# Forming the recurrence's level scores for all blocks of a chunk in one batch per level

## The chip, the cores and the metric

The kernel runs on one core of a Trainium2 chip. The metric is the device time of one execution in microseconds, as the median of several runs. The core has five engines with queues of their own, which run in order and wait for each other by semaphores: PE (TensorE, matrix products, with its weight loads shown as PEld), DVE (VectorE), ACT (ScalarE), POOL (GpSimd) and SP (SyncE, which here issues most DMAs).

## The reference

One layer of a hybrid decoder runs for a prompt of 1024 tokens and a sample group of 8 sequences with 8 new tokens each (64 rows). It is a SwiGLU feed-forward, then a mixer, then another feed-forward. The mixer projects the normed input once and splits the columns between sliding-window attention and a gated linear recurrence (HGRN2) with 4 heads, 128 keys and 128 values. What matters here is the recurrence:

```python
hq = jax.nn.silu(hq)
f = lb + (1.0 - lb) * jax.nn.sigmoid(hf)
o, S = hgrn2_chunked(hq, 1.0 - f, jnp.log(f), hi, s0)
...
def step(S, inp):
    qb, kb, gb, vb = inp
    G = jnp.cumsum(gb, axis=2)
    diff = G[:, :, :, None, :] - G[:, :, None, :, :]
    decay = jnp.exp(jnp.where(causal, diff, -jnp.inf))
    A = jnp.einsum('bhtk,bhsk,bhtsk->bhts', qb, kb, decay)
    o = jnp.einsum('bhts,bhsv->bhtv', A, vb) + jnp.einsum('bhtk,bhkv->bhtv', qb * jnp.exp(G), S)
    G_last = G[:, :, -1:, :]
    S = jnp.exp(G_last[:, :, 0, :])[..., None] * S + jnp.einsum('bhsk,bhsv->bhkv', kb * jnp.exp(G_last - G), vb)
    return S, o
```

So inside a block every query `t` meets every earlier key `s` with the product of the forget gates between them, per key dimension; across blocks a state of 128 x 128 per head is carried.

## The kernel before

The 1088 tokens are cut into three chunks (`WIDTH`): chunk 0 has two prompt blocks of 128 and the 64 sample rows, chunks 1 and 2 have three prompt blocks each (`NPB`). Weights and activations of the large products are split into a high and a low part, and `mm3` (L277 to L281) makes three products of each pair, which is where L279, L280 and L281 come from. The program runs feed-forward 1, the mixer's projection `w_in_units`, the mixer, the output projection `w_out_units` and feed-forward 2, with the chunks staggered.

Work that is small but long in dependence (norms, the attention, the recurrence) is written as generators. `stream` starts one with a rate, `tick` is called between pieces of the large products and advances every running stream by its rate in steps (one step ends at a `yield`), and `need` drains a stream before its result is used. `mixer(n)` (L1495) of chunk `n` alternates between a chain of attention steps and a chain of recurrence steps; its rates are `RM = [0.95, 1.0, 1.3]`. The order on each engine's queue is then made by the framework's scheduler, which places instructions by a simulated time; the queues are fixed in the built program.

The recurrence takes the blocks one after another: `hgrn_block` (L1311), and `sample_hgrn` (L1424) for the sample rows. Both begin with `intra` (L1230), which forms the matrix `At` of scores inside a block. The product of gates between key `s` and query `t` is built up by levels: at level `h` (1, 2, 4, ... 64) the block is cut into pairs of runs of `h` tokens, and queries in the second run of each pair meet keys in the first. `Q` and `K` hold queries and keys scaled so far, and `Ds` the gate products over runs of 1, 2, 4, ... tokens. One step of the ladder is:

- PE: the products of `K` and `Q`. Up to `h = 16` all products inside 32 x 32 diagonal squares are formed (`blocks`, L1245, 4 heads x 4 squares, the tile `lv`), and for `h = 32` and `64` just the rectangles that are wanted (L1274, tile `l`). Before the ladder the diagonal itself is formed from unscaled keys and queries (tile `ld`), together with level 1.
- DVE: `copy_predicated` (L1269) takes from the squares what belongs to level `h` into `C`; then `Q` is scaled (L1285).
- POOL: `K` is scaled (L1287); at the end `C` is copied into `At` (L1280). POOL also makes `Ds` (L1259) and clears `At` (L1241).
- ACT: copies `K` out of the chunk's keys at the start (L1239) and the rectangles into `At` (L1277).

Every step ends at a `yield`. After the ladder the block's keys are transposed (L1323), the output is formed from `At`, the values, `Q` and the state (L1329, L1332), and the state is updated (L1336, L1341).

Tiles come from pools with a fixed count of slots: `big` has 12 slots of 6 KB per partition, and holds the projected `q`, `k`, `f`, `hq`, `v` and `g` of a chunk among others; `t2` has 8 slots of 2 KB, where `Q`, `K` and `D` of a block lie; `At` has one slot and `C` two. PSUM has four banks for large products (`mm`) and four for all else (`ax`).

Of the kernel before, what the change touches and what calls it, by code (L numbers as in the profile page):

```python
# [8 lines left out]
F32 = mybir.dt.float32  # L9
# [36 lines left out]
def tile_step(ctx: ExitStack, tc: tile.TileContext, A: dict, O: list):  # L46
# [996 lines left out]
    def mixing(tp, h):  # L1043
# [16 lines left out]
        Z, KX, VN, MT = {}, {}, {}, {}  # L1060
# [169 lines left out]
        def intra(n, c0, r, top, last_q, res):  # L1230

            z = Z[n]
            f, k, q = [z[i][:, :, c0:c0 + r] for i in ("f", "k", "hq")]
            Q, K, D = t2((P, 4, P)), t2((P, 4, P)), t2()
            V.tensor_tensor(Q[:, :, :r], q, f, op=ALU.mult)
            S.copy(K[:, :, :r], k)  # L1239
            At = tp.tile([P, 4, P], F32, tag="At", bufs=1, name=uid("At"))  # L1240
            G.memset(At, 0.0)  # L1241
            C = tp.tile([P, 4, 32], F32, tag="cm", bufs=2, name=uid("cm"))
            nq = r // 32

            def blocks(s, *pairs):  # L1245
                b5 = axbank(s).rearrange("p (l a t) -> p l a t", l=4, a=4)
                for n_, (x, y) in enumerate(pairs):
                    for a in range(4):
                        for i in range(nq):
                            cs = slice(32 * i, 32 * i + 32)  # L1250
                            PE.matmul(b5[cs, n_, a], x[:, a, cs], y[:, a, cs], start=True, stop=True)  # L1251
                return b5

            Ds, off, h = [f], 0, 1
            while h <= top:
                nx = r // (2 * h)
                Dv = Ds[-1].rearrange("p a (x e) -> p a x e", e=2)
# [3 lines left out]
                h *= 2  # L1261
# [4 lines left out]
            while h <= top:  # L1266
                if h <= 16:
                    b4 = b5[:, 1] if h == 1 else blocks("lv", (K, Q))[:, 0]
                    V.copy_predicated(C[:r], lmask[h][:r].unsqueeze(1).to_broadcast([r, 4, 32]), b4[:r])  # L1269
                else:  # L1270
                    b4 = axbank(f"l{h}").rearrange("p (a t) -> p a t", a=4)
                    for c in range(0, r, 2 * h):
                        for a in range(4):
                            PE.matmul(b4[c:c + h, a, :h], K[:, a, c:c + h], Q[:, a, c + h:c + 2 * h],  # L1274
                                      start=True, stop=True)
                    for c in range(0, r, 2 * h):
                        S.copy(At[c:c + h, :, c + h:c + 2 * h], b4[c:c + h, :, :h])  # L1277
                if h == min(top, 16):
                    for i in range(nq):
                        G.tensor_copy(At[32 * i:32 * i + 32, :, 32 * i:32 * i + 32], C[32 * i:32 * i + 32])  # L1280
                nx = r // (2 * h)
                Qv, Kv = [t[:, :, :r].rearrange("p a (x u) -> p a x u", u=2 * h) for t in (Q, K)]
                Dv = Ds.pop(0).rearrange("p a (x e) -> p a x e", e=2)
                if last_q or h < top:
                    V.tensor_tensor(Qv[:, :, :, h:], Qv[:, :, :, h:], Dv[:, :, :, 0:1].to_broadcast([P, 4, nx, h]),  # L1285
                                    op=ALU.mult)
                G.tensor_tensor(Kv[:, :, :, :h], Kv[:, :, :, :h], Dv[:, :, :, 1:2].to_broadcast([P, 4, nx, h]),  # L1287
                                op=ALU.mult)
                h *= 2
                yield  # L1290
            res += [At, Q, K, Ds[0]]
# [19 lines left out]
        def hgrn_block(n, b):  # L1311
# [6 lines left out]
            res = []  # L1318
            yield from intra(n, c0, P, 64, not first, res)
            At, Q, K, D = res  # L1320
            tb = axbank("kT").rearrange("p (a t) -> p a t", a=4)
            for a in range(4):
                PE.transpose(tb[:, a], K[:, a], ident)  # L1323
# [4 lines left out]
            for a in range(4):  # L1328
                PE.matmul(ob[:, a * P:(a + 1) * P], At[:, a], z["v"][:, b, a * P:(a + 1) * P],  # L1329
                          start=True, stop=first)  # L1330
                if not first:
                    PE.matmul(ob[:, a * P:(a + 1) * P], Q[:, a], st[:, a], start=False, stop=True)  # L1332
# [6 lines left out]
            else:  # L1339
                for a in range(4):  # L1340
                    V.scalar_tensor_tensor(st[:, a], st[:, a], D[:, a], ub[:, a],  # L1341
# [82 lines left out]
        def sample_hgrn():  # L1424
            n, c0, r = 0, 256, NS
            z = Z[n]
            res = []
            yield from intra(n, c0, r, 4, True, res)
            At, Q, K, D = res
            tb = axbank("skT").rearrange("p (a t) -> p a t", a=4)  # L1430
            for a in range(4):
                PE.transpose(tb[:r, a], K[:, a, :r], ident)
# [3 lines left out]
            for a in range(4):  # L1436
# [3 lines left out]
                G.tensor_tensor(qm, Q[:, a, :r].rearrange("p (f t) -> p f t", f=2).unsqueeze(2).to_broadcast(  # L1440
# [312 lines left out]
```

## Time and profile before

| | |
|---|---|
| runs (3) | median 1992.44 us, 1992.08 to 1993.96 |
| profiled execution, first to last instruction | 1991.5 us |
| mean granted TensorE clock of the profiled execution | 0.999 |
| DMA, bytes moved and mean rate | 370.31 MB, 186 GB/s |
| HBM read, written | 284.31 MB, 84.71 MB |

For the profiled execution there is its span alone; the runs' times hold what lies around the span too. The profile counts an instruction as busy from its start to its modelled end, and products of PE overlap, so the start of one to the start of the next tells more of PE than the busy time. A product of two plain float32 operands leaves two records in the trace, one of the high and low parts leaves one. "idle before, releaser" names what the engine waited for.

### The profile page before, as it was taken

To read this page: it belongs to the slowest core of one execution; us is meant where nothing else is said; L and a number is where in the kernel's file an instruction comes from. 1 tells how busy PE (TensorE), PEld (TensorE's weight loads), DVE (VectorE), ACT (ScalarE), POOL (GpSimd) and SP (SyncE) were. 2 spreads that over 40 slices of the span, in tenths; PEclk is the share of its full clock that TensorE was granted. 3 is DMA by queue.
4 is the path that set the end of the run, shared out by engine and by line. 5 is a ranking of instruction groups with operands and counts; after the bars stand their busy time and mean duration, and the time that the engine had idled before them with its cause. 6 is when DMAs were issued, how large, how long until landed. Compare 5 with 4: busy or idle time off the path is not lost.

```text
span 1991.5 us, 34618 instructions
## 1 busy us (share of the span) xinstructions
PE 1978.7 (99%) x13331; PEld 1854.6 (93%) x13331; DVE 1406.9 (71%) x2595; ACT 949.0 (48%) x1736; POOL 178.0 (9%) x244
## 2 busy tenths in 40 slices
PE   9999999999999999999999999999999999999998
PEld 8999999999998987797999898989999999999886
DVE  7686767886558656777667756756887877655667
ACT  5753334444445444445344444756544444444453
POOL 0000000000004101211113311220000000000201
PEclk9999999999999999999999999999999999999999
DMA  8735555755677647766434343527565555677874
GB/s 230 225 107 186 175 170 177 232 196 192 228 243 212 182 138 236 251 169 181 128 104 132 92 138 107 177 90 237 165 210 191 197 183 193 209 232 232 291 262 140
DMA packets 377319, 370.31 MB, mean 186 GB/s; under 512 B 40546, under 2 KB 294321, under 8 KB 377137
## 3 DMA queue, kind: packets, MB, share of 16 engines
q1 hardware_dynamic: 371169, 357.21, 56.9%
q10 hardware_dynamic: 5984, 10.88, 1.6%
q8 instruction: 105, 1.72, 0.4%
q14 instruction: 61, 0.50, 0.1%
HBM read 284.31 MB, written 84.71 MB: 185 GB/s over the span
## 4 chain that ended last, share of the span: by engine, by line
PE 96%; DMA 1%; DVE 1%; ACT 1%; issue 0%; SPq 0%; DVEq 0%; ACTq 0%
PE mm L279 28%; PE mm L280 28%; PE mm L281 28%; PE pv L1219 1%; PE c L281 1%; PE c L279 1%; PE c L280 1%; PE sc L1178 1%; PE pT L1206 1%; PE tr L511 1%; DMA ar<-fa 1%; PE lv L1251 1%; PE l L1274 0%; DMA raw<-in_ffn_w_gu_dram 0%; DMA xt<-in_x_prompt_dram 0%; PE av L1329 0%
## 5 line engine op out<-in xcount | busy, mean ns | idle before, releaser
L279 PE MATMUL mm<-h,wsph 128*128 128x320 f32 (+1 forms) x1280 | 407.3, 319 | 0.0
L280 PE MATMUL mm<-h,wsph 128*128 128x320 f32 (+1 forms) x1280 | 405.3, 317 | 0.0
L281 PE MATMUL mm<-h,wspl 128*128 128x320 f32 (+1 forms) x1280 | 403.6, 317 | 0.0
L258 ACT CAST wsph<-raw 128x1024 fp32r<-128x1024 f32 x200 | 209.1, 1048 | 269.6 <-PE mm L280 213.7
L259 DVE TENSOR_TENSOR wspl<-raw,wsph 128x1024 fp32r<-128x1024 f32 x200 | 247.7, 1240 | 125.3 <-ACT wsph L258 120.7
L258 ACT CAST w<-raw 128x512 fp32r<-128x512 f32 (+1 forms) x218 | 160.3, 740 | 209.2 <-PE mm L280 111.9
L259 DVE TENSOR_TENSOR w<-raw,w 128x512 fp32r<-128x512 f32 (+1 forms) x218 | 185.8, 856 | 87.6 <-ACT w L258 87.1
L279 PEld LDWEIGHTS mm<-h,wsph 128*128 128x128 f32 x1280 | 240.2, 188 | 3.8 <-issue 2.8
L281 PEld LDWEIGHTS mm<-h,wspl 128*128 128x128 f32 x1280 | 239.9, 188 | 2.8 <-issue 2.3
L280 PEld LDWEIGHTS mm<-h,wsph 128*128 128x128 f32 x1280 | 240.5, 188 | 1.5 <-issue 1.1
L279 PE MATMUL mm<-h,w 128*128 128x384 f32 (+1 forms) x720 | 240.3, 335 | 0.6 <-ACT w L258 0.5
L280 PE MATMUL mm<-h,w 128*128 128x384 f32 (+1 forms) x720 | 240.7, 335 | 0.0
L281 PE MATMUL mm<-h,w 128*128 128x384 f32 (+1 forms) x720 | 235.4, 334 | 0.0
L279 PE MATMUL mm<-w,h 128*128 128x512 f32 x462 | 181.1, 395 | 0.6 <-DVE big L975 0.6
L280 PE MATMUL mm<-w,h 128*128 128x512 f32 x462 | 181.3, 392 | 0.0
L281 PE MATMUL mm<-w,h 128*128 128x512 f32 x462 | 179.8, 391 | 0.0
L280 PE MATMUL mm<-big,w 128*128 128x384 f32 x528 | 176.5, 334 | 0.0
L279 PE MATMUL mm<-big,w 128*128 128x384 f32 x528 | 176.3, 334 | 0.0
L281 PE MATMUL mm<-big,w 128*128 128x384 f32 x528 | 176.2, 334 | 0.0
L279 PEld LDWEIGHTS mm<-h,w 128*128 128x128 f32 x720 | 135.0, 188 | 1.3 <-ACT w L258 0.7
L280 PEld LDWEIGHTS mm<-h,w 128*128 128x128 f32 x720 | 135.1, 188 | 0.1
L281 PEld LDWEIGHTS mm<-h,w 128*128 128x128 f32 x720 | 134.7, 188 | 0.1
(363 smaller groups left out, 3576.0 us busy)
## 6 DMA issues: line engine op xcount, KB each, us to landing
raw<-in_ffn_w_gu_dram SPq DMA_DIRECT2D x156, 512.0 KB
raw<-in_ffn_w_down_dram SPq DMA_DIRECT2D x74, 512.0 KB
raw<-in_w_in_dram SPq DMA_DIRECT2D x54, 512.0 KB
ar<-fa SPq DMA_DIRECT2D x70, 384.0 KB
big<-in_ffn_w_down_dram SPq DMA_DIRECT2D x88, 256.0 KB
fb<-big SPq DMA_DIRECT2D x44, 512.0 KB
fa<-big SPq DMA_DIRECT2D x22, 768.0 KB
raw<-fb SPq DMA_DIRECT2D x30, 512.0 KB
```

Of the source, the lines that this page charges most:

```text
L258: S.copy(hi, src)
L259: (lo_eng or V).tensor_tensor(lo, src, hi.bitcast(F32), op=ALU.subtract)
L279: PE.matmul(out, a[0], b[0], start=first, stop=False, skip_group_check=resume)
L280: PE.matmul(out, a[0], b[1], start=False, stop=False, skip_group_check=resume)
L281: return PE.matmul(out, a[1], b[0], start=False, stop=last, skip_group_check=resume).ins
L511: PE.transpose(bank[:, i * P:(i + 1) * P], y[kh][:, i, k * P:(k + 1) * P], ident)
L1178: PE.matmul(banks[g][:, i * 256:i * 256 + wk], zq[64 * g:64 * g + 64, 2 * pr + i, b * P:(b + 1) * P], kx[64 * g:64 * g + 64, k0:k0 + wk], ...
L1206: PE.transpose(bank[:, (i * nk + kb) * P:(i * nk + kb + 1) * P], pt[g][:, i, kb * P:(kb + 1) * P], ident)
L1219: PE.matmul(ob[:, hd * 64:hd * 64 + 64], pT[g][:, (i * nk + kb) * P:(i * nk + kb + 1) * P], vn[:, vb, g * 64:g * 64 + 64], start=kb == 0, ...
L1251: PE.matmul(b5[cs, n_, a], x[:, a, cs], y[:, a, cs], start=True, stop=True)
```

## The change

`intra` is no longer called by each block. It runs once per chunk, as the first item in the mixer's chain of recurrence steps, and leaves its results in `M[n]`, from which the blocks and the sample take their parts. Inside, it works in place: `K` and `Q` are the chunk's own tiles of keys and queries (`z["k"]`, `z["hq"]`), not copies. Each level is done for all blocks: up to `h = 16` one bank holds the 32 x 32 squares of three blocks (48 products in a batch; for chunk 0, 32 for its two prompt blocks and, up to `h = 4`, 8 for the sample rows), one mask copy per height of rows, one scaling of `Q`, one of `K`. For `h = 32` three blocks go into a bank, for `h = 64` two. In the loops of these two levels the position `c` is now inside the head `a`. Level 1 is formed as a batch of its own, one step after the diagonal. `At` and the gate products `D` lie in slots of `big`; `C` has one slot for three blocks.

```diff
-        def intra(n, c0, r, top, last_q, res):
+        def intra(n, res):
-            z = Z[n]
-            f, k, q = [z[i][:, :, c0:c0 + r] for i in ("f", "k", "hq")]
-            Q, K, D = t2((P, 4, P)), t2((P, 4, P)), t2()
-            V.tensor_tensor(Q[:, :, :r], q, f, op=ALU.mult)
-            S.copy(K[:, :, :r], k)
-            At = tp.tile([P, 4, P], F32, tag="At", bufs=1, name=uid("At"))
+            z, w, pw = Z[n], WIDTH[n], NPB[n] * P
+            K, Q, f = [z[i] for i in ("k", "hq", "f")]
+            pool_d = big()
+            D = pool_d.rearrange("p a t -> p (a t)")
+            At = big(F32, (P, 3, 4, P))
             G.memset(At, 0.0)
-            C = tp.tile([P, 4, 32], F32, tag="cm", bufs=2, name=uid("cm"))
+            C = tp.tile([P, 3, 4, 32], F32, tag="cm", bufs=1, name=uid("cm"))
...
+            def parts(h):
+                return [(P, slice(0, 3))] if n else [(P, slice(0, 2))] + ([(NS, slice(2, 3))] if h <= 4 else [])
+            def blocks(s, h):
+                b5 = axbank(s)[:, :384].rearrange("p (b a t) -> p b a t", b=3, a=4)
+                for r, bs in parts(h):
+                    for b in range(bs.start, bs.stop):
+                        for a in range(4):
+                            for i in range(r // 32):
+                                cs = slice(b * P + 32 * i, b * P + 32 * i + 32)
+                                PE.matmul(b5[32 * i:32 * i + 32, b, a], K[:, a, cs], Q[:, a, cs],
+                                          start=True, stop=True)
+                return b5
...
-            b5 = blocks("ld", (k, q), (K, Q))
-            V.tensor_tensor(C[:r], b5[:r, 0], ident32[:r].unsqueeze(1).to_broadcast([r, 4, 32]), op=ALU.mult)
+            b5 = blocks("ld", 1)
+            for r, bs in parts(1):
+                V.tensor_tensor(C[:r, bs], b5[:r, bs], ident32[:r].unsqueeze(1).unsqueeze(1).to_broadcast(
+                    [r, bs.stop - bs.start, 4, 32]), op=ALU.mult)
+            V.tensor_tensor(Q[:, :, :w], Q[:, :, :w], f[:, :, :w], op=ALU.mult)
             yield
-            h = 1
-            while h <= top:
+            for h in reversed(LEVELS):
                 if h <= 16:
-                    b4 = b5[:, 1] if h == 1 else blocks("lv", (K, Q))[:, 0]
-                    V.copy_predicated(C[:r], lmask[h][:r].unsqueeze(1).to_broadcast([r, 4, 32]), b4[:r])
+                    b5 = blocks("lv", h)
+                    for r, bs in parts(h):
+                        nb = 4 * (bs.stop - bs.start)
+                        V.copy_predicated(C[:r, bs].rearrange("p b a t -> p (b a) t"),
+                                          lmask[h][:r].unsqueeze(1).to_broadcast([r, nb, 32]),
+                                          b5[:r, bs].rearrange("p b a t -> p (b a) t"))
...
                 else:
-                    b4 = axbank(f"l{h}").rearrange("p (a t) -> p a t", a=4)
-                    for c in range(0, r, 2 * h):
-                        for a in range(4):
-                            PE.matmul(b4[c:c + h, a, :h], K[:, a, c:c + h], Q[:, a, c + h:c + 2 * h],
-                                      start=True, stop=True)
-                    for c in range(0, r, 2 * h):
-                        S.copy(At[c:c + h, :, c + h:c + 2 * h], b4[c:c + h, :, :h])
...
+                    per = 3 if h == 32 else 2
+                    for b0 in range(0, NPB[n], per):
+                        bs = range(b0, min(b0 + per, NPB[n]))
+                        b4 = axbank(f"l{h}")[:, :per * 4 * h].rearrange("p (b a t) -> p b a t", b=per, a=4)
+                        for b in bs:
+                            for a in range(4):
+                                for c in range(0, P, 2 * h):
+                                    t = b * P + c
+                                    PE.matmul(b4[c:c + h, b - b0, a], K[:, a, t:t + h],
+                                              Q[:, a, t + h:t + 2 * h], start=True, stop=True)
+                        for c in range(0, P, 2 * h):
+                            S.copy(At[c:c + h, b0:bs[-1] + 1, :, c + h:c + 2 * h], b4[c:c + h, :len(bs)])
...
-                if last_q or h < top:
-                    V.tensor_tensor(Qv[:, :, :, h:], Qv[:, :, :, h:], Dv[:, :, :, 0:1].to_broadcast([P, 4, nx, h]),
-                                    op=ALU.mult)
+                V.tensor_tensor(Qv[:, :, :, h:], Qv[:, :, :, h:], Dv[:, :, :, 0:1].to_broadcast([P, 4, nx, h]),
+                                op=ALU.mult)
                 G.tensor_tensor(Kv[:, :, :, :h], Kv[:, :, :, :h], Dv[:, :, :, 1:2].to_broadcast([P, 4, nx, h]),
                                 op=ALU.mult)
...
         def hgrn_block(n, b):
...
-            res = []
-            yield from intra(n, c0, P, 64, not first, res)
-            At, Q, K, D = res
+            At, Q, K, D = [M[n][i] for i in ("At", "Q", "K", "D")]
+            cs = slice(c0, c0 + P)
...
         def sample_hgrn():
...
-            yield from intra(n, c0, r, 4, True, res)
-            At, Q, K, D = res
+            At, Q, K, D = [M[n][i] for i in ("At", "Q", "K", "D8")]
+            At, Q, K, D = At[:, 2], Q[:, :, c0:c0 + r], K[:, :, c0:c0 + r], D[:, :, c0 // 8:(c0 + r) // 8]
...
         def mixer(n):
...
-            hg = [hgrn_block(n, b) for b in range(NPB[n])]
+            M[n] = {}
+            hg = [intra(n, M[n])] + [hgrn_block(n, b) for b in range(NPB[n])]
```

More of the change, by code (lines that the diff above doesn't have):

```diff
@@ L1228, in attn_block @@
             yield from finish_attn(n, o, P, slice(b * P, (b + 1) * P))
[L1230 to L1257 removed]
+        def intra(n, res):
[4 more added lines that the diff above has]
+            At = big(F32, (P, 3, 4, P))
+            G.memset(At, 0.0)
+            C = tp.tile([P, 3, 4, 32], F32, tag="cm", bufs=1, name=uid("cm"))
+            Ds, off = [f[:, :, :w]], 0
+            for h in (1, 2, 4, 8, 16, 32, 64):
+                nx = (w if h <= 4 else pw) // (2 * h)
+                Dv = Ds[-1][:, :, :2 * nx].rearrange("p a (x e) -> p a x e", e=2)
                 Ds.append(D[:, off:off + 4 * nx].rearrange("p (a x) -> p a x", a=4))
@@ new lines, in intra @@
+                    b5 = blocks("lv", h)
[4 more added lines that the diff above has]
+                                          b5[:r, bs].rearrange("p b a t -> p (b a) t"))
+                        if (r, h) in ((NS, 4), (P, 16)):
+                            for i in range(r // 32):
+                                ds = slice(32 * i, 32 * i + 32)
+                                G.tensor_copy(At[ds, bs, :, ds], C[ds, bs])
+                else:
+                    per = 3 if h == 32 else 2
[10 more added lines that the diff above has]
+                            S.copy(At[c:c + h, b0:bs[-1] + 1, :, c + h:c + 2 * h], b4[c:c + h, :len(bs)])
```

33 lines of the change are left out of this document (14 added, 19 removed).

## The prediction

> **What bounds the kernel now.** I read the page first (span, engines, chain), then PE's waits, the groups of the changed lines, and the timeline of PE around single batches.
>
> ```profile
> span 1991.5 us, 34618 instructions
> ...
> PE 1978.7 (99%) x13331; PEld 1854.6 (93%) x13331; DVE 1406.9 (71%) x2595; ACT 949.0 (48%) x1736; POOL 178.0 (9%) x244
> ...
> PE 96%; DMA 1%; DVE 1%; ACT 1%; issue 0%; SPq 0%; DVEq 0%; ACTq 0%
> ```
> ```profile
> PE lv L1251 <- DVE big L1369: 1.1, 1, 1.1
> ```
>
> PE is the chain. All its idle time is 1991.5 - 1978.7 = 12.8 us, and in all the level work it waits once, for 1.1 us. So an edit counts only by what it does to the length of PE's own queue, or by a new wait in it. Here is the part of that queue which the change touches:
>
> ```profile
> L1251 PE MATMUL lv<-t,t 128*32 128x32 f32 x1056 | 15.8, 199 | 1.1 <-DVE big L1369 1.1
> ...
> L1274 PE MATMUL l<-t,t 128*64 128x64 f32 x64 | 5.4, 228 | 0.0
> ...
> L1274 PE MATMUL l<-t,t 128*32 128x32 f32 x128 | 4.7, 199 | 0.0
> L1251 PE MATMUL ld<-big,big 128*32 128x32 f32 x272 | 4.4, 199 | 0.0
> L1251 PE MATMUL ld<-t,t 128*32 128x32 f32 x272 | 4.3, 199 | 0.0
> ```
>
> Each of these products has two records, so there are 528 + 32 + 64 + 136 + 136 = 896. The changed program has the same 896, and the same 12,011 products in all; only their order on PE differs. Before, they come as 59 batches: per block one diagonal batch (two sets of 16), four of 16, one of 8 (h = 32), one of 4 (h = 64), for 8 blocks; and three for the sample. After, each chunk has one batch per step of its ladder, and the built order keeps every batch whole: 18 of up to 48 for L1251, 3 for h = 32, 5 banks in 3 stretches for h = 64.
>
> **What a batch costs.** A batch's price is the time from the start of the last projection product before it to the start of the second one after it (the first still starts into the tail), less two steps of the projection.
>
> ```profile
> 740.15 0.39 PE L281 MATMUL mm<-w,h 128*128 128x512 f32 x1
> 740.47 0.46 PE L1251 MATMUL lv<-t,t 128*32 128x32 f32 x32
> ...
> 741.20 0.39 PE L280 MATMUL mm<-w,h 128*128 128x512 f32 x1
> 741.43 0.40 PE L281 MATMUL mm<-w,h 128*128 128x512 f32 x1
> ```
> ```profile
> 730.22 0.39 PE L281 MATMUL mm<-w,h 128*128 128x512 f32 x1
> 730.54 0.46 PE L1251 MATMUL ld<-big,big 128*32 128x32 f32 x32
> 730.81 0.49 PE L1251 MATMUL ld<-t,t 128*32 128x32 f32 x32
> ...
> 731.58 0.39 PE L280 MATMUL mm<-w,h 128*128 128x512 f32 x1
> ```
>
> One step is 741.43 - 741.20 = 0.23. Sixteen products cost 1.05 - 0.46 = 0.59 us; 32 in a row cost 1.36 - 0.46 = 0.90. So 16 more cost 0.31, and entering and leaving a batch 0.59 - 0.31 = 0.28, whatever its length. The 43 stretches of L1251 (9 diagonal, 34 level) become 18: 25 x 0.28 = **-7.0 us**. The other two kinds:
>
> ```profile
> 831.48 0.39 PE L281 MATMUL mm<-w,h 128*128 128x512 f32 x1
> 831.80 0.59 PE L1274 MATMUL l<-t,t 128*32 128x32 f32 x16
> ...
> 832.66 0.39 PE L280 MATMUL mm<-w,h 128*128 128x512 f32 x1
> ```
> ```profile
> 837.22 0.39 PE L279 MATMUL mm<-w,h 128*128 128x512 f32 x1
> 837.53 0.68 PE L1274 MATMUL l<-t,t 128*64 128x64 f32 x8
> ...
> 838.48 0.39 PE L281 MATMUL mm<-w,h 128*128 128x512 f32 x1
> ```
> ```profile
> 877.68 0.34 PE L280 MATMUL mm<-h,wsph 128*128 128x384 f32 x1
> 877.95 0.45 PE L1251 MATMUL ld<-t,t 128*32 128x32 f32 x16
> ...
> 878.60 0.34 PE L279 MATMUL mm<-h,wsph 128*128 128x384 f32 x1
> ```
>
> At h = 32, 8 products cost 1.18 - 0.46 = 0.72. The old loop runs four heads on one 32-column place and then four on another; the new one (c inside a) alternates. The sample's diagonal alternates between two places too: 8 products, 0.92 less two 384-column steps of 0.17 (an estimate, 0.23 x 384/512) = 0.58. So a product there costs between (0.72 - 0.28)/8 = 0.055 and (0.58 - 0.28)/8 = 0.0375. I take the alternating row, which is the same pattern: 8 x 0.72 = 5.8 becomes 64 x 0.0375 + 3 x 0.28 = 3.2, **-2.5 us** (-1.4 with the other). At h = 64, 4 cost 1.26 - 0.46 = 0.80, or 0.13 each beside 0.28; 8 x 0.80 = 6.4 becomes 32 x 0.13 + 3 x 0.28 = 5.0, **-1.4 us**. PE's queue is shorter by 10.9 us. The bounds are -9.8 (the dearer h = 32) and -12.9, which allows 2 us for the neighbours, transposes and attention products, that come to stand elsewhere and may lose some entries of their own; nothing in the trace sizes that, so I keep -10.9.
>
> **The other engines.** The mask copy, the Q product and the K product run once per step for three blocks instead of three times; the elements are the same (the h = 64 product of Q, once skipped, is added for the first block), so DVE and POOL lose fixed cost, not work. The copies of K on ACT (9) and Q's separate tile vanish. None is on the chain: DVE is 71% busy. The generators also yield less often: the recurrence's ladder takes 8 steps per chunk instead of 8 per block, so the mixer of a chunk has 67, 50 and 51 steps where it had 79, 66 and 67, and at the same rates it ends earlier; that moves the sample's state loads and writes earlier on SP, and nothing on PE waits for a mixer's end today (no such row among PE's waits), so I count 0. What can matter is how late Q and K are ready for the next batch. K, Q and the wait of today:
>
> ```profile
> L1287 POOL TENSOR_TENSOR t<-t,t 128x256 f32<-128x256 f32 x48 | 38.1, 793 | 184.3 <-PE lv L1251 128.6 <-PE l L1274 55.7
> L1287 POOL TENSOR_TENSOR t<-t,big 128x256 f32<-128x256 f32 x8 | 8.6, 1070 | 82.9 <-PE ld L1251 82.9
> ```
> ```profile
> 757.36 0.29 DVE L1269 COPY_PREDICATED cm<-lm,lv 128x128 f32<-128x128 uint8 x1
> 757.56 0.42 DVE L1285 TENSOR_TENSOR t<-t,t 128x256 f32<-128x256 f32 x1
> ```
> ```profile
> 758.12 0.46 PE L1251 MATMUL lv<-t,t 128*32 128x32 f32 x32 [1.06 <-DVE big L1369]
> ```
>
> The 1.06 us wait is such a handoff: Q's product ended at 757.98 behind other DVE work, the batch began at 758.12. With 768 elements for 256, K costs at most 3 x 1.07 = 3.2 us, mask copy and Q at most 3 x (0.29 + 0.42) = 2.1. The built order puts 13 to 35 projection products and up to 16 small ones between two steps of a chunk: by the steps above 4.4 to 6.9 us, 5.7 in the mean (an estimate). Each engine by itself is in time. This cover is gone where DVE or POOL is behind; the order on DVE is as it was, so I leave the one wait of 1.1 in place and **add one more of 1.1 us** (bounds: -1.1, if even the old one goes, and the handoff rival below).
>
> At and the D products move from a tile of their own and the small pool into the 12 big slots. So the sample's key tile (L1369 before) now takes the slot of a state tile and waits, in DVE's queue, until that state is written to HBM; behind it stand the splits of the next weights and of the last activations of the FFN, for which PE waits. The write is queued on SP behind weight loads.
>
> ```profile
> out_dram<-big SPq DMA_DIRECT2D x4, 512.0 KB
> ```
> ```profile
> 860.00:900.00 40.00, 40.00 (x329) 37.85 (x328) 27.46 (x56) 14.43 (x26) 5.03 (x9) 1.00 0.62 181
> ```
>
> 0.52 MB at 181 GB/s is 2.9 us; the built order leaves some 3 us of PE work (thirteen 512-column steps of 0.23) between issue and copy, and DVE has 12.5 us of 40 free. I take 0 (bounds 0 and 6, twice the transfer).
>
> **Sum.** -10.9 + 1.1 = -9.8: span 1991.5 - 9.8 = 1981.7. The runs' median, 1992.44, is 0.9 above this span; so **1982.6 us**. Its own range is 1978 (-12.9 and -1.1) to 1986.
>
> **Rival 1: the handoffs stall (slower).** Speaking for it, DVE and POOL get in each other's way:
>
> ```profile
> 727.48 1.23 DVE L259 TENSOR_TENSOR w<-raw,w 128x1024 fp32r<-128x1024 f32 x1 [0.39 <-ACT w L258]
> ...
> 731.50 1.90 DVE L259 TENSOR_TENSOR w<-raw,w 128x1024 fp32r<-128x1024 f32 x1 [1.96 <-ACT w L258]
> ```
> ```profile
> 731.45 0.86 POOL L1287 TENSOR_TENSOR t<-t,big 128x256 f32<-128x256 f32 x1 [39.51 <-PE ld L1251]
> ```
>
> The same split takes 1.23 us alone and 1.90 started just after a K product. If a split, mask copy, K and Q run one after another, a step needs 1.9 + 0.9 + 3.2 + 1.3 = 7.3 us against 5.7: 1.6 us of wait at each of 21 steps, 34 us. 1991.5 - 10.9 + 34 = 2014.6, with 0.9 about 2015. It decides from 10.9/21 = 0.52 us per step on. Against it: PE now waits at one of some 50 steps, and the queue is rarely that full when a batch ends. Chance 0.09. The Trainium skill (SBUF — State Buffer, Who interferes with whom) has this as a rule: a DVE instruction with two SBUF inputs and a GpSimd one that reads SBUF exclude each other, and the second blocks fully; the two splits above agree with it. By that rule alone K and Q would take turns, which is the part 3.2 + 1.3 of this rival.
>
> **Rival 2: given back in one place.** The key copy's wait blocks DVE for longer than the slack, or chunk borders drift: 6 us at the write-back, and two handoffs of 1.1: 1991.5 - 10.9 + 8.2 + 0.9 = about 1990. For it: untried slots; against: PE has weights ahead. Chance 0.11.
>
> **Rival 3: it merges nothing.** If the 0.28 were the price of 16 products rather than of a batch, 48 would cost 3 x 0.59, and only the h = 32 order is left: about 1990 to 1992. Against it: the pair at 730 us, 0.90 and not 1.18. Chance 0.05.
>
> **Numbers.** Forecast 0.75, rivals 0.09, 0.11, 0.05. About 0.2% (4 us) is what a measurement of this kernel can tell from no change. Faster: 0.75, half of rival 2, and a little of rival 3: 0.81; same 0.10; slower 0.09. The range is 1977 (bounds, a little below) to 1990 (rival 2); rival 1 and the edges are left out.
>
> **What would show it.** PE's span shorter by its queue: after should show 26 batches of ld, lv and l where there were 59 (lv and ld with 64 to 96 records each), a 48-batch of about 1.2 us (0.28 + 3 x 0.31), and no more than two or three waits of PE on DVE or POOL in them. Rival 1 would show as PE waiting for the K or Q product at most steps; rival 2 as one wait of several us near 840 us; rival 3 as a 48-batch of 1.8 us. I am wrong if PE's wait for Q or K exceeds 0.5 us per step.

## The result, and the profile after

| | time, median (us) | span of the profiled run | PE busy | span less PE busy | half clock, end of the run left out |
|---|---|---|---|---|---|
| before | 1992.1 | 1991.5 | 1978.7 | 12.8 | none |
| after | 1996.6 (1995.6 to 1999.1) | 1996.1 | 1977.9 | 18.2 | 3.4 + 13.7 |

The ratio after to before is 1.0025, with a 95% interval of 1.0015 to 1.0036. The forecast was 1982.6 and faster; the kernel is slower by 4.5 us. The two first lines of the page of after and its view of PE's waits (engine, line and tile that waits, what ended the wait; us in total, times, longest):

```profile
span 1996.1 us, 34286 instructions
...
PE 1977.9 (99%) x13331; PEld 1859.0 (93%) x13331; DVE 1405.0 (70%) x2522; ACT 942.3 (47%) x1713; POOL 153.1 (8%) x142
```
```profile
PE pT L1206 <- ACT t L1195: 2.9, 1, 2.9
PE kT L1335 <- POOL big L1299: 2.4, 1, 2.4
PE ax L566 <- DVE sm L570: 1.1, 1, 1.1
PE hT L1318 <- DVE t L1314: 0.9, 1, 0.9
PE tr L468 <- DVE h L473: 0.9, 1, 0.9
PE mm L279 <- ACT big L770: 0.7, 1, 0.7
PE skT L1379 <- DMA kv<-in_cache_k_win_dram: 0.6, 1, 0.6
```

No row has a level batch (`lv`, `l`) waiting for `Q` or `K`. The two long waits are new: the transposes of attention weights (`pT`) wait for an exponential, and those of the first block's keys (`kT`) for the last scaling of `K`. Both stand in the mixer of chunk 2. Behind each of them the granted clock falls to one half, as the view by stretches shows (stretch; its length, then busy time and count of PE, PE's loads, DVE, ACT and POOL; granted clock; DMA):

```profile
1226.95:1230.37 3.42, 1.03 (x13) 0.90 (x11) 1.56 (x2) 0.76 (x3) 2.19 (x1) 1.00 0.53 156
1230.37:1233.78 3.41, 3.41 (x18) 3.41 (x17) 1.71 (x8) 3.38 (x10) 0.00 (x0) 0.50 0.00 0
1295.22:1298.63 3.41, 0.57 (x4) 0.31 (x3) 1.64 (x4) 2.91 (x5) 0.00 (x0) 1.00 0.53 155
1298.63:1312.28 13.65, 13.58 (x48) 10.58 (x49) 3.75 (x14) 7.86 (x21) 0.00 (x0) 0.50 0.17 52
```

In 3.41 + 13.65 = 17.06 us PE is busy and does what takes 8.5 us at the full clock. That is visible in single rows: the eight records of `pv` behind the wait take 1.97 us, eight of the same product at the full clock (in the run with idle steps, below) 1.00. First after, then that run, in the timeline (start, length, engine, line):

```profile
1300.66 1.97 PE L1219 MATMUL pv<-vn,t 128*128 128x64 f32 x8
```
```profile
1305.62 1.00 PE L1219 MATMUL pv<-vn,t 128*128 128x64 f32 x8
```

The batches themselves did what was forecast. A batch of 48 products (96 records) in the timeline of after:

```profile
994.04 0.31 PE L280 MATMUL mm<-h,wsph 128*128 128x320 f32 x1
994.19 0.31 PE L281 MATMUL mm<-h,wspl 128*128 128x320 f32 x1
994.43 1.03 PE L1258 MATMUL lv<-big,big 128*32 128x32 f32 x96
995.38 0.41 PE L279 MATMUL mm<-h,wsph 128*128 128x320 f32 x1
995.64 0.31 PE L280 MATMUL mm<-h,wsph 128*128 128x320 f32 x1
```

From the last projection product before it to the second one after it are 995.64 - 994.19 = 1.45 us; less two steps of 0.15 (994.19 - 994.04) it costs 1.15 us, where 0.28 + 3 x 0.31 = 1.21 was forecast.

One more term is needed for the sums, and the prediction did not have it. The four score products (L1178) of half an attention block are issued by the program together, but the built order often leaves two of them for some microseconds later. In the timeline of before, such a pair (4 records), and a half-block whose four stayed together (8 records):

```profile
786.56 1.13 PE L1178 MATMUL sc<-kx,big 64*128 64x256 f32 x4
787.62 0.50 PE L279 MATMUL mm<-w,h 128*128 128x512 f32 x1
...
809.67 1.13 PE L1178 MATMUL sc<-kx,big 64*128 64x256 f32 x8
810.74 0.50 PE L279 MATMUL mm<-w,h 128*128 128x512 f32 x1
```

Two products alone hold PE for 1.06 us, four together for 1.07. A divided half-block therefore costs 1.05 us more. Of the 14 half-blocks with full windows 6 are divided before, and 7 after.

So the 4.6 us between the spans are: idle time 18.2 - 12.8 = +5.4; half clock +8.5; one more divided half-block +1.05; and what is left of the difference in PE's busy time, (1977.9 - 1978.7) - 8.5 - 1.05 = **-10.4 us, for the batches**, against -10.9 in the prediction. The gain is there, and 15 us elsewhere take it back. This last term is a remainder. The same sum over the other profiled runs with merged batches (below) gives -9.6 to -12.6 us, and -4.8 us for the changed kernel at the scaled rates, which stays unexplained.

Why PE waits there. At 1225.65 the batch of `h = 64` runs, and behind it in PE's queue stand directly the key transposes, with no projection product between. The key scaling that they need is one operation for three blocks. PE, then POOL, in the timeline of after (in brackets the idle time before an instruction and what ended it):

```profile
1225.65 1.61 PE L1289 MATMUL l<-big,big 128*64 128x64 f32 x24
1229.65 0.66 PE L1335 MATMUL kT<-ident,big 128*128 128x128 f32 x4 [2.39 <-POOL big L1299]
```
```profile
1227.41 2.19 POOL L1299 TENSOR_TENSOR big<-big,big 128x768 f32<-128x768 f32 x1 [3.05 <-PE l L1289]
```

The other wait is on a chain of small steps through DVE and ACT. DVE, ACT and PE:

```profile
1291.92 1.75 DVE L501 TENSOR_TENSOR h<-big,h 128x1536 fp32r<-128x1536 f32 x1
...
1294.20 0.16 DVE L1189 SCALAR_TENSOR_TENSOR sm<-sm,sinkb 128x4 f32<-128x4 f32 x1
1294.27 1.22 DVE L259 TENSOR_TENSOR wspl<-raw,wsph 128x1024 fp32r<-128x1024 f32 x1
1295.41 0.16 DVE L1191 TENSOR_SCALAR sm<-sm 128x4 f32<-128x4 f32 x1
```
```profile
1296.75 1.28 ACT L1195 ACT_TABLE_LOAD   x1
1298.04 0.51 ACT L1195 ACTIVATE t<-t,sm 128x256 f32<-128x256 f32 x1
```
```profile
1298.70 2.17 PE L1206 MATMUL pT<-ident,t 128*128 128x128 f32 x8 [2.90 <-ACT t L1195]
```

The maximum of the scores is ready at 1291.92, and then its scaling stands behind the low part of an activation split (L501, 1.75) and a weight split (1.22) on DVE, and the exponential behind a table load (1.28) on ACT. Such things were in these queues before too. What is new is that attention has less of PE's work between its steps. In `both` the two chains of a mixer take turns; the recurrence now has 30, 20 and 20 steps beside 37, 30 and 31 of attention, where it had 42, 36 and 36 (counted in the code). When it is through, attention gets every step. Whether this is the cause is put to the test below.

### The profile page after: what moved, and what is told of

It is laid out like the page before. It is cut to its first block, busy times and chain, and to the rows that moved or that the text cites. A ratio compares the mean times of both kernels' runs of the same rounds, so it can differ in the third digit from the quotient of the medians.

```text
span 1996.1 us, 34286 instructions
## 1 busy us (share of the span) xinstructions
PE 1977.9 (99%) x13331; PEld 1859.0 (93%) x13331; DVE 1405.0 (70%) x2522; ACT 942.3 (47%) x1713; POOL 153.1 (8%) x142
## 4 chain that ended last, share of the span: by engine, by line
PE 96%; DMA 1%; ACT 1%; DVE 1%; issue 0%; POOL 0%; SPq 0%; DVEq 0%; ACTq 0%; POOLq 0%
PE mm L279 28%; PE mm L280 28%; PE mm L281 28%; PE pv L1219 1%; PE sc L1178 1%; PE c L281 1%; PE c L279 1%; PE c L280 1%; DMA raw<-in_ffn_w_gu_dram 1%; PE pT L1206 1%; PE lv L1258 1%; PE tr L511 1%; PE av L1341 0%; PE u L1348 0%; PE av L1344 0%
```

## The experiments

All times are medians; the kernel before, run beside each group, had 1993.0, 1992.6, 1992.0 and 1993.2 us. "Changed" is the kernel after.

### Four ways to mend it

Theory: the gain of the batches is lost where attention comes denser behind the shorter recurrence (the density theory). Rival: the tripled operations on DVE and POOL and their handoffs cost it wherever they stand.

**Idle steps.** In the changed kernel:

```diff
-            gens = list(gens)
-            while gens:
-                for g_ in list(gens):
-                    if next(g_, "end") == "end":
-                        gens.remove(g_)
-                    else:
+            gens, left = list(gens), len(gens)
+            while left:
+                for j, g_ in enumerate(gens):
+                    if g_ is not None and next(g_, "end") == "end":
+                        gens[j], left = None, left - 1
+                    if left:
                         yield
```

> Where one of the two chains of a mixer has ended, an idle step is left in its place, so that attention's steps come as far apart behind the end of the recurrence as beside it. Density theory: the recurrence now has 20 steps against 31 of attention in chunk 2, so attention's last third comes twice as dense, PE waits 2.9 us there for an exponential and then runs 13.7 us at half clock. With the idle steps both go: no PE wait over 1 us at the attention transposes, no half clock between 1290 and 1315 us, about 10 us less, 1986 to 1988; the wait for the last scaling of the keys near 1228 us stays. Rival (the tripled operations on DVE and POOL and their handoffs cost the time wherever they stand): 1995 to 1998.

Measured: 1988.9 us, ratio to before 0.9981 (0.9972 to 0.9989); 7.6 less than the changed kernel. The wait at `pT` and the 13.7 us at half clock are gone, the wait at `kT` (2.4) and the 3.4 us at half clock behind it are still there. The size is a little under the forecast. The profiled run has another 3.4 us at half clock, near 862 us, that the changed kernel has not.

**Two steps before the key transposes.**

```diff
                 yield
+            yield
+            yield
             res.update(At=At, Q=Q, K=K, D=Ds[0], D8=Ds8)
```

> Two empty steps stand between the last level and the transposes of the first block's keys. Density theory: the 2.4 us wait of those transposes for the last scaling of the keys on POOL goes, and with it the 3.4 us at half clock behind it; the attention part stays, so 1991 to 1993. Rival (tripled operations and handoffs in general): 1995 to 1998, the wait only moves to the next consumer.

Measured: 1988.7 us, 0.9979 (0.9969 to 0.9990). The wait at `kT` is gone, but the gain is twice the forecast: the two steps moved attention in chunk 2 as well, its longest `pT` wait is 0.7 us, and the 13.7 us at half clock are gone too. So this run does not isolate `kT`. A new wait took some of the gain back: a transpose of the sample's attention waits 1.5 us near 903 us, and 3.4 us at half clock follow.

**As many steps as before.** Three steps for each level (in chunk 0 two from level 8 on), so that the chains have 42, 36 and 36 steps again:

```diff
-            yield
+            for _ in range(3):
+                yield
...
-                yield
+                for _ in range(3 if n or h <= 4 else 2):
+                    yield
```

> The level steps give way as often as those of the separate blocks did (three times each, in chunk 0 two from level 8 on), so that both chains of each mixer have as many steps as before; operations, batches and places are those of the change. Density theory: both long waits and both stretches at half clock go, and the shorter PE queue shows: 1979 to 1984. Rival (tripled operations, big slots, handoffs): no change, 1994 to 1998.

Measured: 1979.9 us, 0.9933 (0.9921 to 0.9945). This is the theory's number, and the rival falls as it was stated (no change): every tripled operation and every big slot is still there. The padding also gives each handoff three times the room, so this run alone does not part attention's density from the handoffs; the run in proportion, below, bears on that. Two lines of its page, and the longest of PE's waits:

```profile
span 1976.4 us, 34301 instructions
...
PE 1962.4 (99%) x13331; PEld 1848.7 (94%) x13331; DVE 1414.4 (72%) x2522; ACT 948.2 (48%) x1717; POOL 149.1 (8%) x142
```
```profile
PE pT L1206 <- ACT t L1195: 2.7, 2, 2.4
```

Against before, idle time is 14.0 for 12.8 (+1.2), and PE's busy time 1962.4 - 1978.7 = -16.3, with no half clock in either. One half-block of scores is divided where 6 were, -5 x 1.05 = -5.3; the batches are the other **-11.0**. Why the scores stay together here was not tried.

**The last scaling in three.** In the changed kernel, at `h = 64` only:

```diff
+                if h == 64:
+                    for x in range(nx):
+                        G.tensor_tensor(Kv[:, :, x, :h], Kv[:, :, x, :h], Dv[:, :, x, 1:2].to_broadcast([P, 4, h]),
+                                        op=ALU.mult)
...
```

> The scaling of the keys at level 64 is issued on POOL as one operation per block instead of one for three blocks. If the 2.4 us wait of the first block's transposes is the length of that one operation (2.2 us), a third of it is left (under 1 us), the 3.4 us at half clock go, and the time is 1991 to 1993; the attention part stays. If the wait comes from where POOL stands (late start) rather than from the length, the wait stays above 1.5 us and the time at 1995 to 1998.

Measured: 1996.3 us, 1.0018 (1.0009 to 1.0026), no gain. The mechanism held, the time did not. The wait of the transposes (now L1340) is 0.2 us, and the stretch at half clock behind it is gone; but the view by stretches has another one near 862 us, at the sample. No long wait stands right ahead of it: PE has no idle time in the 3.4 us before it.

```profile
PE kT L1340 <- POOL big L1301: 0.2, 1, 0.2
```
```profile
862.25:865.66 3.41, 3.41 (x20) 2.49 (x19) 3.41 (x8) 2.24 (x5) 0.00 (x0) 0.50 0.54 159
```

### What a batch costs, and whether the average pace is enough

**Products by block**, in the kernel with as many steps as before (the calls become `yield from blocks(...)`, and one `yield` follows the diagonal):

```diff
                     for b in range(bs.start, bs.stop):
+                        if b:
+                            yield
...
-                for _ in range(3 if n or h <= 4 else 2):
+                for _ in range(1 if h <= 16 else 3 if n else 2):
```

> The kernel with as many steps as before, but the products of a level up to 16 are issued in one step per block instead of all in one step; everything else on DVE, ACT and POOL stays merged. The built order has 58 stretches of such products where the kernel with the padded steps has 21. If a stretch costs 0.28 us whatever its length (the prediction's batch price), 37 x 0.28 = 10.4 us come back: 1989 to 1991. If the gain came from the other engines' fewer operations or from where the attention products fall, and not from the batches: 1979 to 1983.

Measured: 2000.5 us, 1.0040 (1.0026 to 1.0053), more than the forecast. Its page and its first wait:

```profile
span 1994.2 us, 34315 instructions
...
PE 1976.0 (99%) x13331; PEld 1853.7 (93%) x13331; DVE 1409.2 (71%) x2522; ACT 948.3 (48%) x1717; POOL 145.7 (7%) x142
```
```profile
PE pv L1219 <- DVE t L1209: 4.8, 2, 4.3
```

PE's busy time is 1976.0 - 1962.4 = 13.6 longer; 6.8 us at half clock near 803 us, with PE busy for 6.4 of them, are 3.2 of it, which leaves 10.4, where 37 x 0.28 = 10.4 was expected. The batch price stands. The rest (idle 18.2 for 14.0, and the half clock) comes with new waits, the longest the 4.3 us ahead of the half clock. The profiled execution is the fastest of five (1996.0 us, clock 0.997); the other four have a mean clock of 0.995, so more half clock.

**In proportion.** The changed kernel without added steps; `both` advances the chain that is behind in its share, and the rates are scaled:

```diff
+            chains, done = list(zip(gens, (20 if n else 30, (37, 30, 31)[n]))), [0, 0]
+            live = [0, 1]
+            while live:
+                j = min(live, key=lambda i: (done[i] + 0.5) / chains[i][1])
+                if next(chains[j][0], "end") == "end":
+                    live.remove(j)
+                else:
+                    done[j] += 1
+                    yield
...
-    RM = [0.95, 1.0, 1.3]
+    RM = [0.81, 0.76, 0.99]
```

> No step is added; instead the two chains of a mixer are advanced in proportion to their lengths, and the rates are scaled by the fewer steps (0.81, 0.76, 0.99 for 0.95, 1.0, 1.3), so that a mixer spreads over the same work as before and attention is nowhere denser. Density theory: as good as the padded steps, 1977 to 1983, with no half clock in the mixers. If it is the empty steps themselves that help (handoffs given three times the room): 1988 to 1996.

Measured: 1990.8 us, 0.9990 (0.9981 to 0.9999). A miss for the density theory: attention is nowhere denser in the mean, and still PE waits 4.1 us at a `pT` near 1244 us and 3.0 us at a projection, with 10.2 us at half clock. PE's busy time is short (1967.0), the idle time long (20.3). The number lies in the range of the other theory, that the empty steps help by the room that they give to handoffs. But no level batch and no key transpose waits in this run, so it is not those handoffs that cost here; neither theory has the waits that came.

**Idle steps and two steps together**, by the first two diffs above.

> The idle steps in place of the ended chain and the two empty steps ahead of the first block's key transposes together. If the two long waits are separate losses, both go and the two gains (8 us each against the changed kernel's 1996.6) nearly add: 1981 to 1985. If each of them only shifted attention against the recurrence by some steps, the second adds little: 1987 to 1990.

Measured: 1987.6 us, 0.9971 (0.9961 to 0.9981). The second adds about 1 us to the first. That does not show that the two waits are one loss: the two steps alone had already removed both. What is left are other waits: 2.1 us at a transpose of the sample's attention near 905 us, with 3.4 us at half clock behind it, and 2.1 us at a projection.

**The kernel before, made dense.**

```diff
-                for g_ in list(gens):
-                    if next(g_, "end") == "end":
-                        gens.remove(g_)
-                    else:
+                for g_, m in list(zip(gens, (2, 1))):
+                    for _ in range(m if len(gens) == 2 else 1):
+                        if next(g_, "end") == "end":
+                            gens.remove(g_)
+                            break
                         yield
```

> The kernel before, with its separate blocks and all its steps, but the recurrence takes two steps for one of attention, so that it ends early and the last third of attention comes with nothing between, as in the changed kernel. Density theory: the old kernel then loses time in the same way, PE waits over 2 us for an exponential in chunk 2 and half clock behind it, 1998 to 2004. If the merged operations on DVE and POOL are needed for the loss: 1989 to 1994.

Measured: 2060.7 us, 1.0342 (1.0328 to 1.0356). The direction is the theory's, the size far outside it: the longest wait is 10.0 us, at the transposes of an attention output behind DVE, and level batches wait for DVE and POOL as well, since the recurrence was made denser too. The run shows how much such an order can cost, but not by which of the two.

### The pace

After these misses a second theory stood beside the first: the old rates put the small work where PE happens to wait least, and any shift loses (the tuned pace). Only `RM` is changed, in the kernel before (the first diff; the values of the others are in the table), in the changed one, and in the one with as many steps as before, the padded kernel:

```diff
-    RM = [0.95, 1.0, 1.3]
+    RM = [0.86, 0.9, 1.17]
```

> The kernel before, untouched but for its mixers' rates, a tenth lower (0.86, 0.9, 1.17): attention and recurrence thinner on PE. Density theory: thinner is never worse, 1986 to 1993. Tuned-pace theory (the old rates put the small work where PE happens to wait least, and any shift meets new waits, some of them long enough to halve the clock): 1995 to 2003, with two or more PE waits over 1.5 us that the old pace does not have.

> The kernel before with its mixers' rates a tenth higher (1.05, 1.1, 1.43): denser. Density theory: slower, 1996 to 2004, with waits at the attention transposes. Tuned-pace theory: the same sign, 1995 to 2003; the two differ at the lower rates. If the pace matters little as a whole: 1990 to 1995.

> The changed kernel with its mixers' rates lowered in proportion to the steps that it has lost (0.81, 0.76, 0.99), and the plain alternation of the two chains. Density theory: attention beside the recurrence is thinner than before the change, and its last third still denser; the 2.9 us wait shrinks or goes, 1984 to 1990. Tuned-pace theory: other waits take its place, 1990 to 1998.

> The kernel with as many steps as before (1979.9), the last mixer's rate 1.2 for 1.3. Density theory: its one long wait, 2.7 us at attention transposes near 1222 us, goes and no other comes: 1976 to 1979. Tuned-pace theory: other waits come, 1981 to 1988, since 1.3 was chosen for this order of steps.

| kernel and `RM` | us | ratio to before (95%) |
|---|---|---|
| before, 0.86 0.9 1.17 | 1998.1 | 1.0029 (1.0018 to 1.0039) |
| before, 1.05 1.1 1.43 | 2023.7 | 1.0152 (1.0138 to 1.0166) |
| changed, 0.81 0.76 0.99 | 2004.0 | 1.0058 (1.0045 to 1.0070) |
| steps as before, 0.95 1.0 1.2 | 1976.6 | 0.9925 (0.9911 to 0.9938) |

Neither theory takes all four. The kernel before loses at both sides, as the tuned pace has it, though at the higher rates by 31.6 us, far more than either range; the changed one gets worse than either forecast; but the padded kernel gains where the tuned pace wanted a loss. What the thin side costs is at the mixers' ends. The kernel before at the lower rates, then the changed one at the scaled rates:

```profile
967.88 0.85 PE L279 MATMUL mm<-h,wsph 128*128 128x320 f32 x4 [2.37 <-ACT h L1141]
```
```profile
1345.87 0.84 PE L1154 MATMUL oT<-ident,t 128*128 128x128 f32 x4 [3.52 <-DVE t L1150]
...
1348.50 0.79 PE L279 MATMUL mm<-wsph,h 128*128 128x512 f32 x1 [1.58 <-ACT h L1141]
```

L1141 writes the mixer's last activations: PE waits for a mixer's end, because `need` drains what is left of it just before its result is used. In the changed kernel at the scaled rates the `pT` wait of 2.9 us is indeed gone. So the pace has two bounds, waits inside the mixer when it is dense, and a drained rest when it is thin.

### Where the loss stands, and the control

The padded steps in chunk 2 alone, and in chunks 0 and 1 alone (against the padded kernel; the `yield`s ahead of the ladder get the same condition):

```diff
-                for _ in range(3 if n or h <= 4 else 2):
+                for _ in range(3 if n == 2 else 1):
```
```diff
-                for _ in range(3 if n or h <= 4 else 2):
+                for _ in range(1 if n == 2 else 3 if n or h <= 4 else 2):
```

> The level steps give way as often as before in chunk 2 only; chunks 0 and 1 are those of the change. Place theory: both long waits and all half clock of the changed kernel stand in chunk 2's mixer (1227 to 1312 us), so most of the 16.7 us between the changed and the padded kernel comes back here: 1981 to 1986. If the loss is spread over all chunks in proportion to the steps (24, 16, 16 of 56): 1990 to 1993.

> The complement: the level steps give way as often as before in chunks 0 and 1 only. Place theory: the two long waits of chunk 2 and the half clock behind them stay, 1990 to 1995. If the loss is spread: 1983 to 1987.

Measured: 1986.3 us (0.9968, 0.9955 to 0.9980) and 1993.9 us (1.0004, 0.9995 to 1.0012). Of the 16.7 us between the changed and the padded kernel, chunk 2 alone brings 10.3 and the others 2.7. (The steps that the change took are 12, 16 and 16 of 44, not those of the expectation; spread evenly, chunk 2 would bring 6.1.) With chunks 0 and 1 padded, both waits of chunk 2 stand unchanged:

```profile
PE pT L1206 <- ACT t L1195: 2.9, 1, 2.9
PE kT L1337 <- POOL big L1300: 2.4, 1, 2.4
```

The profiled executions tell what each part brings. With chunk 2 padded, the span is 11.9 us shorter than in the changed kernel: idle time 3.8 less, half clock 6.8 less, two divided half-blocks fewer (5 for 7), 2.1. With chunks 0 and 1 padded it is 4.7 shorter, with the waits and the half clock as they were; four divided half-blocks fewer (3 for 7) are 4.2 of it. So the steps count by a second way, besides the waits: with more of them the built order kept the score products together.

The control for the best version (the kernel before), and the rate bracketed from the other side (the padded kernel):

```diff
-    RM = [0.95, 1.0, 1.3]
+    RM = [0.95, 1.0, 1.2]
```
```diff
-    RM = [0.95, 1.0, 1.3]
+    RM = [0.95, 1.0, 1.1]
```

> Control for the best version: the kernel before with the last mixer's rate 1.2 for 1.3 and nothing else. If the 1976.6 of the padded kernel at this rate comes from the merged batches, the kernel before stays at 1989 to 1999 here. If it is the rate alone, 1978 to 1986.

> The padded kernel with the last mixer's rate 1.1, to bracket 1.2 (1976.6) and 1.3 (1979.9). If the mixer now ends too late, its last steps are drained ahead of the output projection and PE waits there for the mixer's last activations: 1979 to 1986. If slower is simply thinner and better: 1972 to 1976.

Measured: the kernel before with 1.2 for the last mixer has 1996.8 us (1.0017, 1.0008 to 1.0026), so the rate alone brings nothing. The padded kernel with 1.1 has 1976.1 us (0.9915, 0.9902 to 0.9929), the same as with 1.2; a wait of 0.6 us for the mixer's last activations appears, but no loss with it. Both beat the kernel before, by some 16 us, and the changed one by 20.

## Why the prediction was wrong, point by point

- **What bounds the kernel**: right. PE is the chain, and each gain or loss of the runs shows in its busy time, its idle time or its clock.
- **What a batch costs** (-10.9): right in the sum, in part by luck. After has -10.4, the padded kernel -11.0, and giving the batches back by block costs 10.4 for 10.4. But the trace of before has 50 stretches of L1251 and not 43: in five places the diagonal stands some microseconds ahead of level 1, and two stretches are cut. At 0.28 each, the 32 that go would be -9.0 for -7.0. And the price was taken between projection products, as 21 of the 50 stand. Next to other small products a stretch costs less: here 798.56 - 798.17 = 0.39 us for 0.59. The count was too low and the price too high, and the two nearly cancel. From the timeline of before:

```profile
797.65 0.60 PE L1305 MATMUL hT<-ident,t 128*128 128x128 f32 x4
798.17 0.46 PE L1251 MATMUL ld<-big,big 128*32 128x32 f32 x32
798.56 1.09 PE L1206 MATMUL pT<-ident,t 128*128 128x128 f32 x8
...
804.17 0.46 PE L1251 MATMUL ld<-t,t 128*32 128x32 f32 x32
```

- **"... it ends earlier ...; and nothing on PE waits for a mixer's end today (no such row among PE's waits), so I count 0"**: this is the step that failed. The fewer steps were looked at for when a mixer ends, and not for what they do inside it: the two chains take turns by steps, so a shorter recurrence leaves attention with less of the projections between its own steps. Restoring the number of steps, and nothing else, brings 1996.6 to 1979.9, and 10.3 of these 16.7 us come from chunk 2, where the two long waits stand. Between the two profiled spans (19.7 us), idle time is 4.2, half clock 8.5, and six divided half-blocks fewer 6.3. That the fewer steps are the cause is shown; that they act on the waits by how dense attention stands is argued from the waits of chunk 2, and the run in proportion shows that it is not the whole. That no row showed a wait for a mixer's end was true only of the old pace: at slightly lower rates the row is there (2.37 us).
- **The handoffs** ("one more of 1.1 us"): mis-sized and at the wrong place. The next batch never waits for `Q` or `K`. The consumer that the list of PE work between two steps left out is the first key transpose, which follows the last batch with nothing between; it waits 2.4 us.
- **The clock**: absent from the sum. A wait was priced at its length; here two waits of 5.3 us together cost another 8.5 in the stretches behind them.
- **The score products**: the bound of -12.9 allowed 2 us for neighbours "that come to stand elsewhere". In after they cost 1.05 (one more half-block divided), in the padded kernel they bring 5.3.
- **Big slots**: near 850 us PE waits 0.9 and 0.6 us at the sample, not 6. **Rival 2** (given back in one place) is nearest in kind; but the place is chunk 2's mixer and not the sample's write-back, and with the clock it takes back more than the whole gain.
- **Rival 1** (each handoff stalls) and **rival 3** (nothing is merged): out, by the rows of waits and by the 48-batch.

With the steps kept, the span moves by 1976.4 - 1991.5 = -15.1 us: -11.0 for the batches, -5.3 for the scores, +1.2 of idle time. The first and the last are close to the -10.9 and +1.1 of the prediction. The last is luck: the idle time stands at attention's transposes, not at a handoff of the levels. And that the 2.4 us wait of the padded kernel brings no half clock hangs on where it falls (last section).

What stays open: why the proportional order, which has the old mean pace without padded steps, loses most of the gain in other waits. The runs show that the mean density of attention does not decide alone; which distance does was not isolated.

## What to carry to other kernels

Where small work is woven into large work by steps, the number of steps is a part of the schedule: an edit that merges operations should keep the yields, or be tried with padded ones before it is judged. After such an edit, look for the consumer that follows the last merged operation directly, since it now waits for the whole of it. And price a wait of the matmul engine at more than its length: in these runs, about 2 us of idle time within one period of 3.4 us halved the clock of the next (see the next section).

## What the runs showed of the hardware

All stretches at half clock (the end of the run left out) begin and end on a grid of 3.413 us that runs through the whole execution, and last one to five of its periods. What counts is how much of one period PE is idle, not the length of the wait. In the changed kernel, the period 1226.95 to 1230.37 holds all of the 2.39 us wait (PE busy 1.03 of 3.42), and the next one is at 0.50. The padded kernel has a wait as long, 2.44 us, but an edge of its grid cuts it:

```profile
1220.24:1223.65 3.41, 2.07 (x104) 1.77 (x102) 3.41 (x10) 2.09 (x3) 1.19 (x1) 1.00 0.42 157
1223.65:1227.06 3.41, 2.25 (x15) 2.00 (x16) 3.31 (x10) 2.96 (x10) 0.40 (x1) 1.00 0.70 213
1227.06:1230.47 3.41, 3.41 (x26) 3.40 (x25) 3.41 (x6) 3.14 (x9) 0.00 (x0) 1.00 0.84 294
```

The two periods have 1.34 and 1.16 us idle, and the clock stays. With chunk 2 alone padded the same wait (2.45 us, at a `pT`) falls into one period, and the clock does not stay:

```profile
1229.01:1232.43 3.42, 0.97 (x80) 0.77 (x66) 3.35 (x10) 1.68 (x5) 1.58 (x1) 1.00 0.38 107
1232.43:1235.84 3.41, 3.38 (x15) 3.17 (x14) 3.38 (x7) 3.38 (x12) 0.00 (x0) 0.50 0.76 238
```

Between 700 and 1500 us, over all the profiled runs, every period with 1.8 us or more idle was followed by the half clock, and none of those with 0.7 to 1.46 us idle that began at the full clock; of the eight between, at 1.52 to 1.69 us, two were followed by it and six were not. The Trainium skill (TensorE: Matmul & The Clock Gate, What's actually happening) has the free-running window of 3413 ns and the half clock after an idle window. The trace agrees with the grid, but a period did not have to be idle throughout. The Trainium skill warns on that page (TensorE: Matmul & The Clock Gate, Why this matters for your kernels) of gaps over some 3 us. Here 2.1 to 2.4 us were enough when they fell into one period. Four stretches at half clock follow periods with under 0.1 us of idle time, at the sample's small products (near 862 us with the idle steps and with the last scaling in three, near 926 us in the changed kernel at the scaled rates, near 959 us in the kernel before at the higher ones); why is open. Why the stretch of 13.65 us lasted four periods with PE busy is open too.
